# A streaming encoder layer on one core: column blocks in pairs by Strassen's algorithm, side work between the products

## The chip, the cores and the metric

The kernel runs on one core of one Trainium2 chip. The metric is the device time of one execution in microseconds. The engines are called as in the profile: PE is TensorE, DVE is VectorE, ACT is ScalarE, POOL is GpSimd, SP issues the DMAs.

## The reference

One layer of a hybrid encoder for 1088 tokens (1024 of a new stream, 64 of a running one) of width 1024. The rows of `P` are tokens; its 10,248 columns are the inputs, gates and merge gates of four branches.

```python
h = rms_norm(x, p['norm_pre'])
proj = h @ p['w_in']
lru_x, lru_g, ssd_z, ssd_xbc, ssd_dt, cf_in, cf_g, sb_qkv, sb_g, merge = split_cols(proj, IN_SPLITS)
# A: RG-LRU: causal conv of 4, two block-diagonal gates, h_t = a_t h_{t-1} + b_t; u_a = lru_h * silu(lru_g)
# B: SSD: conv of 4, silu, scan in chunks; u_b = rms_norm(y * silu(ssd_z))
# C: glu = cf_in[..., :CF_W] * sigmoid(cf_in[..., CF_W:]); conv of 31; LayerNorm; u_c = silu(...) * silu(cf_g)
# D: stick-breaking attention over the past; u_d = o * silu(sb_g)
u = jnp.stack([u_a, u_b, u_c, u_d], axis=2)
y_br = jnp.einsum('btnc,ncd->btnd', u, p['w_down'])
gates = jax.nn.sigmoid(merge.reshape(bsz, t, N_BRANCH, D_MODEL))
mixed = jnp.sum(gates * y_br, axis=2)
out = rms_norm(mixed @ p['w_out'], p['norm_post'])
return x + out, new
```

Each branch is 512 wide; `w_down` is 512 x 1024 per branch, `w_out` 1024 x 1024. The states of the scans and convolutions and k, v are outputs too.

## The kernel before

Activations lie with channels on partitions and tokens along the free axis. Every large product is done in fp32r in three parts: an operand is split into a high part (`split`: a rounding copy on ACT) and a low part (the difference, on DVE), and `mm3` (L104 to L107) adds high x high, high x low and low x high. `w_in` without dt is 80 blocks of 128 columns; `weights` (L90) loads one block of 512 KB and splits it, and `project` multiplies it with h in three pieces of tokens (`SPL`: 256, 384, 448), 24 matmuls in each piece. `proj` is that as a generator: it yields after each piece. A down product (`down`) has 12 matmuls per piece.

The order of PE is the order of the code (a manual schedule holds for PE alone); the other engines are ordered by a scheduler with priorities. A `Feed` holds generators of matrix work, and `feed.step(n)` issues n pieces of it between two steps of another chain, so that PE has something to do while that chain runs on DVE and ACT. In this order:

- head: RMSNorm of x, transposes, split into `hh` and `hl` (resident), with the first V blocks between;
- the convolution module's inputs and the attention: 68 units (`Unit.scores`, `turn`, `output`), with 18 pieces of projection per column group of k and q between them. The convolution of 31 taps runs on DVE (`conv`, L239) beside it;
- RG-LRU and the inputs of SSD (`lru_scan`, `ssd_x_chunk`), with projections between;
- LayerNorm of the convolution module (L714 on) in three pieces: mean by a ones matmul (L761), square, variance by a ones matmul (L769), root, reciprocal, scale, sigmoid, products, split, store. Between the steps stand 2 pieces of `merge` each, and `lnx` has two buffers. A piece of `merge` is a gate projection (24 matmuls) and a down product (12);
- SSD in 9 chunks (`Chunk.first` to `fourth`), pipelined over chunks: the third and fourth step of a chunk stand beside the first and second of the next, with 5 pieces of `merge` per chunk;
- the gates of the last branch (1) alone, its down products, then the output projection with RMSNorm.

`merge` computes m = sum of gate x down for the branches in the order 3, 0, 2, 1. Scratch in DRAM holds the split u of each branch (`uh_d`, `ul_d`), which `load_u` brings back in six pieces. L435 is a causal mask on POOL in the attention, L438 its scan, L439 the product after it. L742 are dt's transposes and L745 to L752 the chain from there to `adt`. L617 to L632 is `lru_scan`.

## Time and profile before

| | us |
|---|---|
| median of three runs (1494.28 to 1495.47) | 1494.86 |
| span of the profiled execution | 1490.9 |
| PE busy | 1460.1 |
| DVE busy | 921.1 |
| ACT busy | 588.5 |
| POOL busy | 118.9 |

The span is that of one profiled execution, from its first instruction to its last; the runs are timed around it. Busy time of PE is that of overlapping matmuls, so that the starts of neighbouring matmuls tell their spacing, and their durations don't. A row of a timeline has the start and the duration in us, then engine, line, operation, output <- inputs and the shape; "[a <-b]" is idle time of the engine before it and what ended that.

### The profile page before, as it was taken

How to read it: one execution, taken by the hardware profiler on the slowest of the kernel's cores; microseconds unless marked ns; L12 is line 12 of the kernel's file. 1: busy time of each engine (PE TensorE's matmuls, PEld its weight loads, DVE VectorE, ACT ScalarE, POOL GpSimd, SP SyncE). 2: the span in 40 equal slices, each digit the busy share in tenths (PEclk: the TensorE clock that was granted, in tenths of full speed). 3: DMA queues.
4: the chain of work that ended last, by engine and by line, in shares of the span. 5: the costliest groups of instructions: out<-in, count | busy, mean ns of one | idle time of the engine just before them, and what ended most of it. 6: DMA issues, size and time to landing. Idle time of an engine off the chain costs nothing.

```text
span 1490.9 us, 23008 instructions
## 1 busy us (share of the span) xinstructions
PE 1460.1 (98%) x9157; PEld 1360.5 (91%) x9157; DVE 921.1 (62%) x1379; ACT 588.5 (39%) x1000; POOL 118.9 (8%) x157
## 2 busy tenths in 40 slices
PE   6999999999999999999999999999999999999997
PEld 5898999999999998999999999999999999999885
DVE  6289589579769955677765554656655541019433
ACT  6323434443453344666644322333332332124211
POOL 0003212231221222000000000000000000000000
PEclk9999999999999999999999999999999999999999
DMA  6232212313212323454433354222621234113322
GB/s 209 75 87 63 72 61 68 103 44 89 92 46 87 98 87 109 138 117 107 116 124 116 110 169 142 82 68 83 196 78 57 75 88 148 51 43 113 99 85 71
DMA packets 103339, 144.17 MB, mean 97 GB/s; under 512 B 20800, under 2 KB 82112, under 8 KB 103232
## 3 DMA queue, kind: packets, MB, share of 16 engines
q1 hardware_dynamic: 103232, 142.71, 31.9%
q8 instruction: 72, 1.18, 0.3%
q14 instruction: 35, 0.29, 0.1%
HBM read 97.95 MB, written 40.53 MB: 93 GB/s over the span
## 4 chain that ended last, share of the span: by engine, by line
PE 87%; issue 6%; DVE 4%; DMA 1%; ACT 1%; POOL 1%; SPq 0%; DVEq 0%; POOLq 0%; ACTq 0%
PE pj L105 24%; PE pj L106 24%; PE pj L107 24%; PE pg L468 2%; PE pg L450 2%; PE pg L106 1%; PE pg L107 1%; PE pg L105 1%; DVE cvo L239 1%; PE pz L417 1%; PE pz L418 1%; PE pg L878 1%; PE pg L736 1%; PE pg L871 1%; DMA g_bc<-in_npre_dram 0%
## 5 line engine op out<-in xcount | busy, mean ns | idle before, releaser
L105 PE MATMUL pj<-hh,w_hi 128*128 128x384 f32 (+2 forms) x1920 | 637.6, 332 | 1.7 <-ACT hh L220 1.7
L106 PE MATMUL pj<-hl,w_hi 128*128 128x384 f32 (+2 forms) x1920 | 631.8, 329 | 1.8 <-DVE hl L221 1.8
L107 PE MATMUL pj<-hh,w_lo 128*128 128x384 f32 (+2 forms) x1920 | 631.5, 329 | 0.0
L105 PEld LDWEIGHTS pj<-hh,w_hi 128*128 128x128 f32 x1920 | 363.6, 189 | 16.6 <-issue 2.1
L106 PEld LDWEIGHTS pj<-hl,w_hi 128*128 128x128 f32 x1920 | 363.7, 189 | 14.4 <-DVE hl L221 2.6
L107 PEld LDWEIGHTS pj<-hh,w_lo 128*128 128x128 f32 x1920 | 363.5, 189 | 11.0
L98 DVE TENSOR_TENSOR w_lo<-w_raw,w_hi 128x1024 fp32r<-128x1024 f32 x96 | 117.5, 1224 | 226.9 <-ACT w_hi L97 226.7
L97 ACT ACTIVATE w_hi<-w_raw 128x1024 fp32r<-128x1024 f32 x96 | 101.7, 1060 | 281.7 <-PE pj L106 262.6
L239 DVE SCALAR_TENSOR_TENSOR cvo<-cbuf,p_t,cvo 128x1118 f32<-128x1118 f32 x120 | 165.6, 1380 | 2.1
L105 PE MATMUL pj<-uh,w_hi 128*128 128x384 f32 (+2 forms) x384 | 126.2, 329 | 0.0
L107 PE MATMUL pj<-uh,w_lo 128*128 128x384 f32 (+2 forms) x384 | 126.2, 329 | 0.0
L106 PE MATMUL pj<-ul,w_hi 128*128 128x384 f32 (+2 forms) x384 | 126.1, 328 | 0.0
L438 DVE TENSOR_TENSOR_SCAN fb<-fb,ones 128x128 f32<-128x128 f32 (+8 forms) x68 | 90.0, 1324 | 38.0 <-POOL fb L435 37.4
L435 POOL TENSOR_SCALAR_AFFINE_SELECT beta<-beta 128x128 f32<-128x128 f32 (+1 forms) x72 | 78.2, 1086 | 14.4 <-ACT beta L431 13.7
L698 DVE TENSOR_TENSOR sg<-pj,sg 128x256 f32<-128x256 f32 (+2 forms) x48 | 25.7, 535 | 84.9 <-PE pj L107 80.6
L689 ACT ACTIVATE sg<-pj 128x256 f32<-128x256 f32 (+2 forms) x72 | 33.7, 468 | 112.2 <-PE pj L107 112.0
L105 PEld LDWEIGHTS pj<-uh,w_hi 128*128 128x128 f32 x384 | 72.7, 189 | 2.3
L106 PEld LDWEIGHTS pj<-ul,w_hi 128*128 128x128 f32 x384 | 72.6, 189 | 2.2
L107 PEld LDWEIGHTS pj<-uh,w_lo 128*128 128x128 f32 x384 | 72.6, 189 | 2.2
L435 POOL TENSOR_SCALAR_AFFINE_SELECT fb<-fb 128x128 f32<-128x128 f32 (+1 forms) x72 | 38.2, 530 | 449.2 <-ACT fb L430 354.4
L439 DVE TENSOR_TENSOR beta<-beta,fb 128x128 f32<-128x128 f32 (+8 forms) x68 | 50.3, 740 | 4.3 <-POOL beta L435 0.7
L452 ACT ACTIVATE wT<-pg 128x512 f32<-128x512 f32 (+3 forms) x96 | 43.3, 485 | 18.1 <-PE pg L450 17.8
(313 smaller groups left out, 1683.0 us busy)
## 6 DMA issues: line engine op xcount, KB each, us to landing
w_raw<-in_win_dram SPq DMA_DIRECT2D x80, 512.0 KB, 3.7
w_raw<-in_wdn_dram SPq DMA_DIRECT2D x16, 512.0 KB, 3.6
xt<-in_x_dram SPq DMA_DIRECT2D x8, 512.0 KB, 10.5
xbc<-xs SPq DMA_DIRECT2D x8, 512.0 KB, 2.6
xb<-xbc SPq DMA_DIRECT2D x8, 512.0 KB, 4.9
w_raw<-in_wout_dram SPq DMA_DIRECT2D x8, 512.0 KB, 3.7
xr<-in_x_dram SPq DMA_DIRECT2D x8, 512.0 KB, 3.8
out_y_dram<-yo SPq DMA_DIRECT2D x16, 256.0 KB, 2.3
```

The costliest lines, as they stand in the source:

```text
L97: S.activation(hi, r3, AF.Copy)
L98: V.tensor_sub(lo, r3, hi.bitcast(FT))
L105: PE.matmul(out, ah, bh, start=first, stop=False)
L106: PE.matmul(out, ah, bl, start=False, stop=False)
L107: PE.matmul(out, al, bh, start=False, stop=last)
L239: V.scalar_tensor_tensor(out[:, :n], b[:, i:i + n], w[:, i:i + 1], out[:, :n], op0=OP.mult, op1=OP.add)
L435: G.affine_select(t_[s, 1024 - w:1024], t_[s, 1024 - w:1024], pattern=[[-1, w]], compare_op=OP.is_gt, fill=fill, base=0, channel_multiplier=1)
L438: V.tensor_tensor_scan(F[:, rev], F[:, rev], ones[:, 0:1].to_broadcast([128, n]), 1.0, OP.mult, OP.mult)
L439: V.tensor_tensor(B[:, L:1024], B[:, L:1024], F[:, L + 1:1025], op=OP.mult)
L450: PE.transpose(p[:, (j - j0) * 128:(j - j0 + 1) * 128], B[:, L + j * 128:L + (j + 1) * 128], ident)
L452: S.activation(wT[:, j0:j1, :], p[:, :(j1 - j0) * 128].rearrange("p (j c) -> p j c", c=128), AF.Copy)
L689: S.activation(sg[:, :n], p[:, :n], AF.Sigmoid)
```

## The change

**The products.** 38 pairs of column blocks (76 of the 80; all but V) are multiplied by Strassen's algorithm in Winograd's form: h is cut in four quarters (512 rows by 544 tokens), the weights of a pair into four (512 rows by 128 columns), and 7 products of a sum of weights with a sum of h take the place of 8. The sums of h are made once at the start, by DVE, and split (`quad_parts`). The sums of weights are made on POOL for each pair (`prepare`, 4 instructions), and each of the 7 weights is split (`split_w`). A product is 2 quarters of 272 tokens with 12 matmuls of 272 columns; its sums gather in PSUM banks (`bank`, 6 of them) and in two SBUF tiles R, by copies on ACT and additions on DVE. When a pair is done, `done` applies its activation and stores it to DRAM scratch; all gates are stored too (`mg_d`).

**The order.** V and dt come first, with dt's chain up to the cumulative sums (`acs`) right after them. Then 22 pairs with the inputs of all branches and the convolutions; then 16 pairs of merge gates (`NP` on), and after each of their 112 products one step of a single chain: RG-LRU in 8 items of half a channel block (17 steps), LayerNorm in 4 quarters of 272 tokens (12), SSD in 9 chunks of six steps (54), not pipelined. All tiles of these steps have one buffer, among them `xl`, `lnx`. Then the attention, with its q, k, v and gate loaded from scratch (`Head`), and between its units the 72 pieces of down products of branches 0, 2 and 1, whose gates are loaded; from the second branch on POOL adds the product to m. Last the down products of branch 3 (attention) and the output projection, as before.

The diff, cut to its core:

```diff
-LNA, LNB = (2, 2, 2), 5
...
+NSLOT, NR = 5, 3
+PV = ((0, 256), (256, 288), (544, 256), (800, 288))
...
+    V.tensor_sub(h12, h12, h11)
+    V.tensor_sub(h22, h22, h12)
+    quad_parts(6, h22)
+    V.tensor_sub(h11, h22, h11)
+    quad_parts(5, h12)
+    quad_parts(7, h11)
+    V.tensor_sub(h21, h21, h22)
+
...
+        split(hi, lo, src)
+        quad[j] = hi, lo
...
+    class Pair:
+
+
+        def __init__(self, c0, c1, done, last=AF.Copy):
+            self.chunks, self.done, self.last, self.src = (c0, c1), done, last, None
+
+        def prepare(self):
+            if self.src is not None:
+                return
+            raw = load_w(*self.chunks)
+            a11, a12, a21, a22 = raw[:, 0, 0], raw[:, 0, 1], raw[:, 1, 0], raw[:, 1, 1]
+            s1, s2, s4 = (wp.tile([128, 4, 128], FT, name=f"s{j}", bufs=1) for j in (1, 2, 4))
+            with tc.high_priority(offset=W_PRIO):
+                G.tensor_tensor(s1, a21, a22, op=OP.add)
+                G.tensor_tensor(s2, s1, a11, op=OP.subtract)
+                G.tensor_tensor(a21, a11, a21, op=OP.subtract)
+                G.tensor_tensor(s4, a12, s2, op=OP.subtract)
+            self.src = {1: a11, 6: s2, 2: a12, 7: a21, 5: s1, 4: a22, 3: s4}
...
+        def run(self, weights, between):
+            R = [ru.tile([128, T], FT, name="r", bufs=NR) for _ in range(2)]
+            banks = {}
+            for j in ORDER:
+                hi, lo = weights()
+                bh, bl = quad[j]
+                for q in range(2):
+                    key = {2: "b", 5: "c", 3: "c"}.get(j, "a"), q
+                    new = j in (1, 2, 5)
+                    if new:
+                        banks[key] = bank()
+                    p = banks[key][:, :QT]
+                    s = slice(q * QT, q * QT + QT)
+                    for k in range(4):
+                        for z, (a_, b_) in enumerate(((hi, bh), (hi, bl), (lo, bh))):
+                            PE.matmul(p, a_[:, k], b_[:, k, s], start=new and k == 0 and z == 0, stop=k == 3 and z == 2,
+                                      skip_group_check=True)
...
+                    with tc.high_priority(offset=C_PRIO):
+                        if j == 1:
+                            S.activation(r11, p, AF.Copy)
+                        elif j == 2:
+                            V.tensor_tensor(r11, p, r11, op=OP.add)
+                        elif j == 6:
+                            S.activation(r12, p, AF.Copy)
+                        elif j == 5:
+                            S.activation(r22, p, AF.Copy)
+                        elif j == 7:
+                            V.tensor_tensor(r22, p, r22, op=OP.add)
+                        elif j == 3:
+                            V.tensor_tensor(r12, p, r12, op=OP.add)
+                        else:
+                            S.activation(r21, p, self.last)
+                between()
+            self.done(R)
...
+            G.tensor_tensor(b[:, 30:TP + 30], R[0][:, :TP], R[1][:, :TP], op=OP.mult)
+            G.tensor_tensor(b[:, TP + 60:WC], R[0][:, TP:], R[1][:, TP:], op=OP.mult)
...
+    pairs = [cf(0), lx(0), q_(0), k_(0), sx(0), cf(1), lx(2), q_(2), k_(2), sx(2), cf(2), sx(4), DG[0], LG[0], cf(3), sx(6),
+             DG[1], LG[1], SZ[0], SZ[1], CG[0], CG[1]]
+    NP = len(pairs)
+    pairs += [gated(C_MG, AF.Sigmoid, mg_d, 2 * i) for i in range(16)]
...
+        for q in range(4):
+            t = slice(q * QT, q * QT + QT)
+            X = ln.tile([128, 4, QT], FT, name="lnx")
+            gl = ln.tile([128, 4, QT], FT, name="lng")
+            dma(X, cv_d[:, :, t])
+            dma(gl, cg_d[:, :, t])
+            a = fold(X)
+            yield
+            p = pg()[:, :QT]
+            PE.matmul(p, ones, a, start=True, stop=True)
+            V.scalar_tensor_tensor(X, p[:, None, :].to_broadcast([128, 4, QT]), -1.0 / 512, X, op0=OP.mult, op1=OP.add)
+            sq = ln.tile([128, 4, QT], FT, name="lnq")
+            S.activation(sq, X, AF.Square)
+            a = fold(sq)
...
+            gh = ln.tile([128, 4, QT], FR, name="lnh", tag="lnq")
+            gw = ln.tile([128, 4, QT], FR, name="lnl", tag="lng")
+            split(gh, gw, X)
+            dma(uh_d[2][:, :, t], gh.bitcast(FT))
+            dma(ul_d[2][:, :, t], gw.bitcast(FT))
+            yield
...
+                xc = lp.tile([128, HT], FT, name="xl")
+                dma(xc, xl_d[:, c, t])
+                g = lp.tile([128, HT], FT, name="lg_t")
+                dma(g, lg_d[:, c, t])
+                xh, xl = (lp.tile([128, HT], FR, name=f"xg{f}") for f in range(2))
+                split(xh, xl, xc)
+                gr = lp.tile([128, HT], FT, name="gr")
+                gx = lp.tile([128, HT], FT, name="gx")
+                yield
+                for t0 in (0, QT):
+                    for dst, w, bias in ((gr, bd[0], P("ba", c)), (gx, bd[1], P("bx", c))):
+                        p = pg()[:, :QT]
+                        mm3(p, w[0][:, c, :], w[1][:, c, :], xh[:, t0:t0 + QT], xl[:, t0:t0 + QT], True, True)
+                        S.activation(dst[:, t0:t0 + QT], p, AF.Sigmoid, bias=bias)
+                    if t0 == 0:
+                        yield
+                ga = lp.tile([128, HT], FT, name="ga")
+                S.activation(ga, gr, AF.Exp, scale=lm8[:, c:c + 1])
...
+    def between_products():
+        yield from lru()
+        yield from layer_norm()
+        yield from ssd()
+        while True:
+            yield
+
+    for n, pair in enumerate(pairs):
+        if n == NP:
+            a3.close()
+            side = between_products()
+        count = [0]
+
+        def between(n=n, count=count):
+            count[0] += 1
+            ahead(3)
+            if count[0] == 2 and n + 1 < len(pairs):
+                pairs[n + 1].prepare()
+            if n >= NP:
+                next(side)
+        pair.run(next_weights, between)
...
+        raw = wp.tile([128, 1024], FT, name="w_raw3", bufs=1)
+        dma(raw, src)
...
+    order = (0, 2, 1, 3)
...
+                if bi == 0:
+                    V.tensor_tensor(m, p[:, :n], gi, op=OP.mult)
+                else:
+                    V.tensor_tensor(gi, p[:, :n], gi, op=OP.mult)
+                    G.tensor_tensor(m, m, gi, op=OP.add)
...
-            xl = ln.tile([128, 4, NM], FT, name="lnx", bufs=2)
-            gl = ln.tile([128, 4, NM], FT, name="lng", bufs=1)
...
-    prev = None
-    feed.step(LNB)
-    for i in range(9):
-        ch = Chunk(i)
-        ch.first()
-        if prev:
-            prev.third()
-        feed.step(2)
-        if prev:
-            prev.fourth()
-        feed.step()
-        ch.second()
-        feed.step(2)
-        prev = ch
-    prev.third()
...
-    for d in range(8):
-        feed.add(proj(C_MG + 8 * b + d, act_to(sga[d], AF.Sigmoid)))
-    feed.drain()
```

Two places in the order of instructions. DVE in the LayerNorm, from the reciprocal of one piece to the start of the next; before, the second piece of 384 tokens, with `L98` the splits of weights and `L696` a merge product:

```order
L772 RECIPROCAL lnr<-lnr 128x384 [waits Activation_49]
L773 TENSOR_TENSOR lnx<-lnx,lnr 128x4x384 [waits DVE_49]
L98 TENSOR_TENSOR w_lo<-w_raw,w_hi 128x1024 [waits DMAHW7_49,PE_49,Activation_49]
L775 TENSOR_SCALAR lnx<-lnx,p_t 128x384 [waits DVE_49]
L775 TENSOR_SCALAR lnx<-lnx,p_t 128x384 x2
L98 TENSOR_TENSOR w_lo<-w_raw,w_hi 128x1024 [waits DMAHW4_49,PE_49,Activation_49]
L775 TENSOR_SCALAR lnx<-lnx,p_t 128x384
L696 TENSOR_TENSOR m_7504<-pj,sg 128x448
L777 TENSOR_TENSOR lnx<-lnx,lnq 128x4x384 [waits Activation_49]
L696 TENSOR_TENSOR m_7505<-pj,sg 128x256 [waits PE_49,Activation_49]
L778 TENSOR_TENSOR lnx<-lnx,lng 128x4x384 [waits DMAHW3_49,DVE_49]
L225 TENSOR_TENSOR lng<-lnx,lnh 128x4x384 [waits DMAHW1_49,Activation_49]
```

Now, from the second quarter of 272 tokens to the third; `L92` with `w_lo` are the splits of product weights, and `L522` is the fold of the next quarter, which waits for its load:

```order
L545 RECIPROCAL lnr<-lnr 128x272 [waits Activation_49]
L92 TENSOR_TENSOR w_lo<-w_raw,w_hi 128x512 [waits PE_49,Activation_49]
L546 TENSOR_TENSOR lnx<-lnx,lnr 128x1088 [waits DVE_49]
L548 TENSOR_SCALAR lnx<-lnx,p_t 128x272 [waits DVE_49]
L548 TENSOR_SCALAR lnx<-lnx,p_t 128x272 x3
L92 TENSOR_TENSOR w_lo<-w_raw,w_hi 128x512 [waits PE_49,Activation_49]
L550 TENSOR_TENSOR lnx<-lnx,lnq 128x1088 [waits Activation_49]
L551 TENSOR_TENSOR lnx<-lnx,lng 128x1088 [waits DMAHW7_49,DVE_49]
L92 TENSOR_TENSOR lnl<-lnx,lnh 128x1088 [waits DMAHW5_49,Activation_49]
L522 TENSOR_TENSOR lns<-lnx 128x544 [waits DMAHW4_49]
L523 TENSOR_TENSOR lns<-lns 128x272 [waits DVE_49]
L536 SCALAR_TENSOR_TENSOR lnx<-pg_7856,lnx 128x1088 [waits PE_49]
```

The next piece's fold (`lns<-lnx`, before L727, now L522) stood ahead of the reciprocal; now it stands behind the last split and a load. On PE, 146 matmuls stand between L769 and the next L761 of before, and 48 between L542 and the next L535 now.

SP's queue ahead of a down product; before, the pieces of branch 1's u, between loads of gate weights:

```order
L662 DMA ul_11871<-ul_74 128x4x384 [waits DMAHW2_49,PE_49]
L662 DMA uh_11869<-uh_70 128x4x384 [waits DMAHW3_49,PE_49]
L92 DMA w_raw<-in_win_dram 128x1024 [waits DMAHW4_49,DVE_49]
L662 DMA uh_11873<-uh_70 128x4x448 [waits DMAHW5_49,DMAHW0_49,PE_49]
L662 DMA ul_11875<-ul_74 128x4x448 [waits DMAHW6_49,DMAHW1_49]
L92 DMA w_raw<-in_win_dram 128x1024 [waits DMAHW7_49,DVE_49]
L92 DMA w_raw<-in_win_dram 128x1024 [waits DMAHW4_49,DVE_49]
L92 DMA w_raw<-in_win_dram 128x1024 [waits DMAHW7_49,DVE_49]
L92 DMA w_raw<-in_win_dram 128x1024 [waits DMAHW2_49,DMAHW0_49,DVE_49]
```

Now, the end of the queue from the last gate's store (23 issues ahead of `w_raw`; the first twelve and more are q, k and vT of the attention):

```order
L881 DMA q_s<-q_83 128x64 [waits DMAHW6_49]
L882 DMA k_s<-k_84 128x64 [waits DMAHW7_49]
L886 DMA vT_11738<-vs 128x1088 [waits DMAHW0_49]
L819 DMA ul_11742<-ul_67 128x4x384 [waits DMAHW1_49,PE_49]
L819 DMA uh_11744<-uh_63 128x4x384 [waits DMAHW2_49,Pool_49]
L819 DMA ul_11746<-ul_67 128x4x384 [waits DMAHW3_49]
L819 DMA uh_11748<-uh_63 128x4x320 [waits DMAHW4_49]
L819 DMA ul_11750<-ul_67 128x4x320 [waits DMAHW5_49]
L801 DMA w_raw_11752<-in_wdn_dram 128x1024 [waits DMAHW6_49]
L825 DMA gate<-mgs 128x1088 [waits DMAHW7_49]
L825 DMA gate<-mgs 128x1088 [waits DMAHW0_49]
```

The down weights (L801) stood among weight loads, each issued ahead of its need; the first of them now stands behind all loads of the attention and of u, which wait for PE's last product.

## Rows read from the trace of the kernel before

**Rows 1.** The page: span, busy time by engine, GB/s in 40 slices, chain
```profile
span 1490.9 us, 23008 instructions
...
PE 1460.1 (98%) x9157; PEld 1360.5 (91%) x9157; DVE 921.1 (62%) x1379; ACT 588.5 (39%) x1000; POOL 118.9 (8%) x157
...
GB/s 209 75 87 63 72 61 68 103 44 89 92 46 87 98 87 109 138 117 107 116 124 116 110 169 142 82 68 83 196 78 57 75 88 148 51 43 113 99 85 71
...
PE 87%; issue 6%; DVE 4%; DMA 1%; ACT 1%; POOL 1%; SPq 0%; DVEq 0%; POOLq 0%; ACTq 0%
```

**Rows 2.** Timeline of TensorE from 1230 us: start, duration, instruction
```profile
1230.29 0.34 PE L107 MATMUL pj<-uh,w_lo 128*128 128x384 f32 x1
...
1231.50 0.36 PE L105 MATMUL pj<-hh,w_hi 128*128 128x448 f32 x1
...
1238.93 0.28 PE L105 MATMUL pj<-hh,w_hi 128*128 128x256 f32 x1
...
1241.45 0.28 PE L105 MATMUL pj<-hh,w_hi 128*128 128x256 f32 x1
```

**Rows 3.** Groups of VectorE by shape: busy us, mean ns, idle before
```profile
L239 DVE SCALAR_TENSOR_TENSOR cvo<-cbuf,p_t,cvo 128x1118 f32<-128x1118 f32 x120 | 165.6, 1380 | 2.1
...
L225 DVE TENSOR_TENSOR uol<-yz,uoh 128x512 fp32r<-128x512 f32 x8 | 5.4, 679 | 0.0
```

**Rows 4.** Timeline of VectorE from 935 us, in a chunk of SSD
```profile
947.58 0.42 DVE L698 TENSOR_TENSOR sg<-pj,sg 128x256 f32<-128x256 f32 x1 [1.62 <-PE pj L107]
...
948.38 0.94 DVE L918 RECIPROCAL rs__9271<-rs__9271 128x128 f32<-128x128 f32 x1
949.36 1.14 DVE L920 SCALAR_TENSOR_TENSOR yz<-yz,p_t,rs__9271 128x128 f32<-128x128 f32 x4
```

**Rows 5.** Instructions of line 435 on GpSimd: ns min/median/max, first and last start
```profile
L435 POOL TENSOR_SCALAR_AFFINE_SELECT beta<-beta x72: 237/1312/2337, 116.9 to 580.4; 128x128 f32<-128x128 f32 x64, 64x64 f32<-64x64 f32 x8
```

**Rows 6.** Groups of GpSimd by shape
```profile
L808 POOL MEMSET Sb<- 128x512 f32 x2 | 1.0, 526 | 295.0 <-DVE lng L225 295.0
```

**Rows 7.** Timelines of TensorE and VectorE, the dt chain
```profile
763.68 1.02 PE L742 MATMUL pg<-ident,dtr 16*128 16x16 f32 x9
...
775.25 0.07 DVE L752 MEMSET adt<- 64x8 f32 x1
```

**Rows 8.** Timelines of TensorE and VectorE, one LayerNorm piece
```profile
817.65 0.81 PE L769 MATMUL pg<-lns,ones 128*128 128x384 f32 x2
...
835.70 1.76 DVE L225 TENSOR_TENSOR lng<-lnx,lnh 128x1536 fp32r<-128x1536 f32 x1 [1.61 <-ACT lnh L224]
```

**Rows 9.** DMA issues: destination, count, KB each, median us to landing
```profile
lg_t<-lg SPq DMA_DIRECT2D x4, 544.0 KB, 3.9
...
lnx<-cv SPq DMA_DIRECT2D x1, 768.0 KB, 7.4
```

**Rows 10.** Timelines of ScalarE and VectorE, RG-LRU of one block
```profile
621.24 0.56 ACT L617 ACTIVATE gx<-pg,p_t 128x364 f32<-128x364 f32 x1
...
627.38 1.28 ACT L622 ACT_TABLE_LOAD   x1
...
627.83 2.75 DVE L239 SCALAR_TENSOR_TENSOR xc<-abuf,p_t,xc 128x1092 f32<-128x1092 f32 x2
...
631.70 1.35 DVE L239 SCALAR_TENSOR_TENSOR xc<-abuf,p_t,xc 128x1092 f32<-128x1092 f32 x1
...
639.46 1.30 DVE L225 TENSOR_TENSOR al<-gx,ah 128x1092 fp32r<-128x1092 f32 x1
```

**Rows 11.** Timeline of SP's issues while branch 1's pieces are loaded
```profile
1231.52 0.57 SPq L662 DMA_DIRECT2D ul<-ul  x1
```

**Rows 12.** The page's costliest groups: scans and products of attention
```profile
L438 DVE TENSOR_TENSOR_SCAN fb<-fb,ones 128x128 f32<-128x128 f32 (+8 forms) x68 | 90.0, 1324 | 38.0 <-POOL fb L435 37.4
...
L439 DVE TENSOR_TENSOR beta<-beta,fb 128x128 f32<-128x128 f32 (+8 forms) x68 | 50.3, 740 | 4.3 <-POOL beta L435 0.7
```

**Rows 13.** Busy time in stretches, granted clock, DMA share, GB/s
```profile
0.00:50.00 50.00, 33.38 (x205) 30.24 (x206) 28.08 (x58) 28.03 (x52) 1.19 (x8) 0.97 0.50 171
```

More of the change, by code (lines that the diff above doesn't have):

```diff
@@ L6 @@
 from contextlib import ExitStack
-from itertools import zip_longest
 FT = mybir.dt.float32
@@ new lines, in encoder_step @@
+    for q in range(4):
+        p = pg()
+        s = slice(q % 2 * QT, q % 2 * QT + QT)
+        for k in range(8):
+            for e, b in enumerate((Bh, Bl)):
+                PE.matmul(p[:16, :QT], wd2[:, k, :], b[q // 2][:, k, s], start=k == 0 and e == 0, stop=k == 7 and e == 1)
+        S.activation(dtr[:, q * QT:q * QT + QT], p[:16, :QT], AF.Copy)
+    quad_parts(4, h21, Bh[1][:, k0], Bl[1][:, k0])
+    pd = pg()
+    for i in range(9):
+        r = 128 if i < 8 else 64
+        PE.transpose(pd[:r, i * 16:i * 16 + 16], dtr[:, i * 128:i * 128 + r], ident[:16, :16])
@@ L927, in encoder_step @@
[L927 to L945 removed]
+        u.turn()
+        if k == NU - 1:
+            u.output(None)
+    feed.drain()
+    p1.close()
     b = order[3]
```

1242 lines of the change are left out of this document (582 added, 660 removed).

## The prediction

> **What bounds the kernel now.** I read the page's busy line first, then its chain, then single instructions, then the stages that the change rebuilds. TensorE is busy for 1460.1 us of a span of 1490.9 us, and 87% of the chain that ended last is TensorE [rows 1]. So before, time is the number of matmuls times their spacing, and the side work (convolutions, RG-LRU, LayerNorm, SSD, attention) costs only what isn't covered. The three runs have a median of 1494.86 us, 4 us above the span; I forecast the span and add 4.
>
> The spacing is read from starts, not from durations, since matmuls overlap: 7 steps of 384 columns take 1.21 us, 36 steps of 448 columns 7.43 us, 21 steps of 256 columns 2.52 us [rows 2]. That is 0.173, 0.206 and 0.120 us, each 13 to 20 ns over columns divided by 2.4 GHz. A column block is 24 matmuls of each width, 24 x 0.499 = 12.0 us, and a pair of blocks 24.0 us.
>
> **The products.** A Strassen pair has 7 products x 2 quarters x 12 matmuls of 272 columns: 168 matmuls in place of 144. The nearest row is 256 columns, so 272/2.4 GHz + 13 to 20 ns = 0.127 to 0.133 us. I take the lower, by the nearer row: 24 x 0.127 = 3.06 us for a product and 21.4 us for a pair. 38 x (24.0 - 21.4) = 97 us saved; by the upper end 62 us. The plain V blocks and dt change TensorE by about +1.5 us. Net **-96**.
>
> **Phase A, 22 pairs and the convolutions (471 us of TensorE).** VectorE now has, per pair, 7 weight splits of 512 (0.68 us) and 6 additions of 272 (0.42 us by a 256-column one [rows 4]); together 7.3 us [rows 3]. The convolutions are 156 x 1.38 = 215 us as before [rows 3], and stand in the first 16 pairs. Up to there VectorE needs 215 + 16 x 7.3 + 10 (q and k splits) = 342 us against 16 x 21.4 = 342 us of TensorE: no slack. On top come 4 additions per pair on GpSimd, of two SBUF operands each, which before has nowhere. What the trace shows of GpSimd beside VectorE: the same select takes 0.24 us at least and 2.34 us at most [rows 5], which I read as waiting for a running VectorE instruction; whether VectorE waits in turn no row shows. A GpSimd instruction over 512 elements takes at least the 0.53 us of a memset [rows 6]; for the upper end I choose twice that, 1.1, since an addition reads two operands where the memset reads none. If VectorE stands still for all of it, the 64 additions of the first 16 pairs cost 34 to 70 us; if for none, 0. Later convolutions may slip into the last 6 pairs (low priority), which takes some back. I take **+30**, range 0 to 75.
>
> The Trainium skill, "SBUF — State Buffer", section "Who interferes with whom", says that a VectorE instruction with two SBUF inputs and a GpSimd instruction that reads SBUF exclude each other for the whole instruction; the spread of the select agrees for one side. "GPSIMD Engine Reference", section 3.1, has 4497 ns for a GpSimd addition of 2048 elements; a quarter of that, as an estimate, is 1.12 us for 512; with it phase A would be at about +60 and the sum 30 higher.
>
> **H to A.** The dt chain now stands with nothing between: transposes, softplus, cumulative sums. Before, the transposes start at 763.68 and the last step of dt ends at 775.32 [rows 7], 11.6 us with other work between its steps; I take off some 5 us of that and add about 2.5 for the cumulative sums that follow. **+9**, range 5 to 12.
>
> **Phase B, 16 gate pairs and the side steps.** There are 112 gaps between products and one side step in each, so 3.06 us of TensorE stands beside each step, and the steps' tiles have one buffer. The price of a step is its chain less the products beside it.
> *LayerNorm.* Before, one piece of 384 tokens takes from the matmul at 817.65 to the end of the last split at 835.70 + 1.76, 19 us after the matmul has ended at 818.46 [rows 8], hidden behind 146 matmuls of other work. A quarter of 272 is 272/384 of that, 13.5 us; then the next load can begin (one lnx buffer): 768 KB take 7.4 us [rows 9], 272/384 of it 5.2; and 1.2 us of folding. 19.9 us, and between L542 and the next L535 stand two products, 6.1 us. 13.8 x 3 quarters = 41. Entering from RG-LRU (its last split, then fold) 12, leaving to SSD, whose first VectorE rows stand behind the LayerNorm's last, 13.
> *RG-LRU.* The chain of before runs from 621.24 to 640.76 for 1092 columns, with 2.6 us of two table loads and 4.1 us of convolution in it [rows 10]; half of the rest is 6.4 us for 544 columns. Now three table loads stand in it (3.8), and a load of 256 KB into the only xl (544 KB take 3.9 us [rows 9]; 3.5 taken, and 0.6 to issue it) with its split (0.7), which stands ahead of the square root on ScalarE: 15.0. Between the gates of two items stand two products and 12 small matmuls, 7.7 us. 7.3 x 7 = 51 us, and 5 to start.
> *SSD.* One product between stages. From the norm's root to the last split before: 0.4 + 0.94 + 1.14 + two splits of 0.68 [rows 3, 4]; with the lt multiplication (0.68) that needs their tiles, a table load and hops it is 5.9 against 3.06: 2.8. The stage before it (transpose, two products of 0.68, square, two folds) 5.2: 2.2. With 0.4 elsewhere 5.4 x 9 = 48, 45 taken.
> Sum of B: 41 + 25 + 56 + 45 = **+167**, range 80 to 250 (below 80 only if the chains run at half of what the rows say).
>
> **B to C.** On SP the last gate store is followed by 24 issues up to the first down weights, all on one queue: u pieces, 12 attention loads, vT, then w_raw3. At 0.57 us each [rows 11] 14 us pass before w_raw3 is issued; the bytes are 9.3 MB, and the fullest slice moved 209 GB/s [rows 1], 44 us. The first down product needs all of this but part of u. Between 14 + 4 and 44 I take **+30**. **C to D:** branch 3 is now last, and its u pieces are stored, then loaded behind the last attention output, where before 96 us of gate projections covered that: a store and a load of 768 KB, by the 7.4 us of another load of that size [rows 9]: **+8**.
>
> **Phase C, attention with 72 down steps.** TensorE has 144 us of down products and about 143 us of attention. VectorE has 90 + 50 us of scans and products [rows 12], 38 of mixes, 15 of weight splits and outputs, 213 in all; GpSimd has its selects and 48 new additions. If these shut out VectorE for 0.5 to 1.1 us each, VectorE stays under TensorE's 287, but the units' chain scan, select, transpose has two pg buffers for three. **+20**, range 0 to 50.
>
> **The sum.** 1490.9 - 96 + 30 + 9 + 167 + 30 + 8 + 20 = 1659, plus 4 around the span: 1663 us. The output projection stays as it is. The head's new sums and splits of h (8 VectorE instructions of 2176 columns, by a 512-column one at 0.68 us about 2.9 us each at most, 23 us) stand beside 24 us of V blocks, so nothing is put down for them; without that cover they are 23.
>
> **Rivals.**
> 1. *Faster: the steps hide.* VectorE is at 62% and ScalarE at 39% [rows 1]; if the chains, without the weight splits that I scaled along, fit beside the products, B costs only its entries, 30, A and C nothing: 1491 - 96 + 9 + 30 + 30 + 8 + 4 = 1476. It is faster than 1492 only if everything outside the products sums to less than 93 us. Against: LayerNorm alone has 13.8 us a quarter uncovered by rows, and one buffer forbids starting early.
> 2. *GpSimd and VectorE stop each other for the whole of every addition,* as the spread of the select would have it: A at +75 and C at +50, 1663 + 75 = 1738.
> 3. *The clock.* With TensorE busy for 33.38 of 50 us the granted clock was 0.97 [rows 13], the level of 2.4 GHz. B would have it busy for 343 of 510 us, the same share. If it falls there to the level of 1.2 GHz, a product takes 24 x (0.227 + 0.013) = 5.8 us, and the waits shrink by what the products grow: 112 x 5.8 = 650 instead of 343 + 167, +140 at most, 1803. No row shows such a fall.
> 4. *The product is dearer,* 0.133 us a matmul: +35, 1698; inside the range.
>
> **How the numbers follow.** Forecast with its own spread (A 0 to 75, B 100 to 230, the others at their ends): 1565 to 1755, chance 0.69. Rival 1: 0.11 faster than 1492, 0.03 between 1492 and 1498, about what a measurement of this kernel can't tell from no change (0.2%). Rival 2 beyond the forecast's terms 0.10, rival 3 0.05, and 0.02 for gaps that hide half. The predicted time is the forecast's, 1663. The range, 1545 to 1765, leaves out rival 1, rival 3 and the tails. Faster 0.11, same 0.03, slower 0.86.
>
> **What would show it.** In the new trace: matmuls of a product 0.127 us apart (0.133 speaks for rival 4); phase A in 22 equal periods of 21.4 us if VectorE keeps up, longer in the first 16 if not, with GpSimd additions of 0.5 us or of 1.1 and more; waits of TensorE before L535, released by VectorE's lns, three of about 13 us; before the gate matmuls of RG-LRU about 6 us each, released by xg; in SSD before the cumulative and the norm matmul; one gap of 20 to 45 us before the first down product, ended by a DMA. Wrong it would be above all if B's waits sum to under 60, or if the granted clock falls.

## The result: 19% slower

The changed kernel takes 1779.76 us (median of 4 runs, 1776.26 to 1780.79), the kernel before 1494.57 (4 runs). The ratio is 1.190, with a 95% interval of 1.1885 to 1.1919. The forecast was 1663 us with a range of 1545 to 1765: the direction was right, the time lies above the range.

The page of the changed kernel, the lines that answer to [rows 1] and the granted clock in 40 slices:

```profile
span 1777.4 us, 26555 instructions
...
PE 1448.0 (81%) x10209; PEld 1363.0 (77%) x10209; DVE 1139.4 (64%) x1675; ACT 774.3 (44%) x1385; POOL 428.9 (24%) x365
...
PEclk9989999999999979766799888899599899989999
...
PE 48%; DVE 21%; issue 13%; ACT 7%; DMA 6%; POOL 3%; SPq 1%; DVEq 0%; POOLq 0%; ACTq 0%
```

PE's busy time is hardly less (1448.0 against 1460.1 us), although the products need some 110 us less (worked out below): at the lower clock the same matmul is busy for longer. PE now makes 48% of the chain that ended last, where it made 87%. The clock digits fall to 6 and 7 in the middle of the program and to 5 after it; in the kernel before they are

```profile
PEclk9999999999999999999999999999999999999999
```

What PE waited for, in us in total, times, and the longest (before, the longest list entry was 10.0 us in the head, and the next 2.4):

```profile
PE pg L535 <- DVE lns L523: 71.5, 4, 20.4
PE pg L676 <- DVE lt L667: 47.2, 10, 12.8
PE pj L86 <- ACT w_hi L91: 37.3, 1, 37.3
PE pg L951 <- DVE ud L983: 30.9, 16, 4.2
PE bank L394 <- DVE r L408: 29.1, 20, 3.8
PE pg L747 <- DVE yt L744: 19.4, 7, 3.7
PE pg L86 <- ACT xg L91: 19.3, 7, 3.8
PE pg L86 <- ACT gr L613: 9.6, 7, 2.3
...
PE pg L343 <- DVE adt L319: 7.6, 1, 7.6
PE pj L87 <- DMA ul<-ul: 7.5, 5, 2.5
PE pj L86 <- DMA uh<-uh: 6.1, 3, 3.7
```

L535 is the mean of LayerNorm, L676 and L747 are in SSD, L86 with xg and gr are RG-LRU's gates, L86 with w_hi is the first down product, L951 the attention's transposes, L394 the products themselves. The stages in one table (starts from PE's timeline: first and last matmul of the products, first down product), us:

| run | before the pairs | 22 pairs (A) | 16 gate pairs (B) | gap to the first down product | the rest | median |
|---|---|---|---|---|---|---|
| changed kernel | 99.6 | 507.4 | 637.3 | 37.5 | 495.6 | 1779.8 |
| filled waits (e1) | 102.2 | 506.1 | 615.7 | 37.0 | 489.3 | 1755.7 |
| two LayerNorm buffers (e2) | 99.6 | 506.8 | 620.0 | 37.3 | 493.7 | 1757.4 |
| down loads first (e3) | 100.8 | 507.0 | 638.2 | 9.1 | 521.1 | 1777.6 |
| additions on DVE (e4) | 105.7 | 465.4 | 624.9 | 37.4 | 477.8 | 1709.6 |
| plain products (e5) | 98.1 | 533.5 | 615.2 | 36.9 | 475.3 | 1761.2 |
| steps after the products (e6) | 101.6 | 507.1 | 336.6, then 402.4 with the gap | | 509.4 | 1858.9 |
| PSUM as before (e7) | 101.7 | 506.5 | 637.9 | 39.2 | 474.9 | 1759.0 |
| e4, gaps given out (e8) | 102.6 | 465.4 | 557.8 | 37.0 | 477.4 | 1645.3 |
| e8, steps first in the queues (e9) | 103.9 | 465.1 | 530.0 | 37.0 | 474.8 | 1615.0 |
| steps begin earlier (e10) | 104.6 | 537.5 | 448.5 | 8.8 | 492.8 | 1593.9 |
| e10, steps first in the queues (e11) | 103.3 | 528.8 | 439.3 | 7.8 | 495.1 | 1576.7 |

In e10 and e11 the last five of the 22 pairs already have side steps beside them, so their column A is not that of the others.

Busy time by engine, granted clock, DMA share and GB/s in A, B and the gap:

```profile
core 0: us, PE busy (x) PEld busy (x) DVE busy (x) ACT busy (x) POOL busy (x), PEclk, DMA share, GB/s
99.60:607.00 507.40, 477.82 (x3699) 472.84 (x3699) 437.59 (x516) 228.36 (x420) 190.80 (x95) 0.98 0.29 103
607.00:1244.60 637.60, 462.92 (x3234) 439.06 (x3232) 351.01 (x586) 302.07 (x477) 87.26 (x63) 0.85 0.30 99
1244.60:1281.80 37.20, 0.00 (x0) 0.00 (x0) 0.01 (x1) 1.44 (x2) 0.00 (x0) 0.55 1.05 317
```

In B, PE is at a mean granted clock of 0.85, and in the gap the DMA engines are full (317 GB/s).

### The profile page after: what moved, and what is told of

The parts are those of the page before. It is cut to its first block, busy times and chain, and to the rows that moved or that the text cites. A ratio compares the mean times of both kernels' runs of the same rounds, so it can differ in the third digit from the quotient of the medians.

```text
span 1777.4 us, 26555 instructions
## 1 busy us (share of the span) xinstructions
PE 1448.0 (81%) x10209; PEld 1363.0 (77%) x10209; DVE 1139.4 (64%) x1675; ACT 774.3 (44%) x1385; POOL 428.9 (24%) x365
## 4 chain that ended last, share of the span: by engine, by line
PE 48%; DVE 21%; issue 13%; ACT 7%; DMA 6%; POOL 3%; SPq 1%; DVEq 0%; POOLq 0%; ACTq 0%
PE bank L394 29%; DVE u L145 7%; PE pj L87 3%; PE pj L88 3%; PE pj L86 3%; DVE w_lo L92 3%; ACT w_hi L91 1%; PE pg L87 1%; POOL beta L936 1%; PE pg L86 1%; PE pg L88 1%; DMA lnx<-cv 1%; DMA ul<-ul 1%; POOL fb L936 1%; POOL m L852 1%
## 5 line engine op out<-in xcount | busy, mean ns | idle before, releaser
L394 PE MATMUL bank<-Bh,w_hi 128*128 128x272 f32 x1216 | 370.4, 305 | 29.1 <-DVE r L408 29.1
L394 PE MATMUL bank<-Bl,w_hi 128*128 128x272 f32 x1216 | 363.1, 299 | 0.0
L394 PE MATMUL bank<-Bh,w_lo 128*128 128x272 f32 x1216 | 362.0, 298 | 0.0
L394 PE MATMUL bank<-Th,w_hi 128*128 128x272 f32 x912 | 272.9, 299 | 0.4 <-ACT r L400 0.4
L394 PEld LDWEIGHTS bank<-Bh,w_hi 128*128 128x128 f32 x1216 | 242.6, 199 | 35.9 <-DVE r L408 33.7
L394 PE MATMUL bank<-Tl,w_hi 128*128 128x272 f32 x912 | 269.9, 296 | 0.0
L394 PE MATMUL bank<-Th,w_lo 128*128 128x272 f32 x912 | 268.9, 295 | 0.0
L145 DVE SCALAR_TENSOR_TENSOR u<-u,p_t 128x1118 f32<-128x1118 f32 (+1 forms) x156 | 247.4, 1591 | 10.4 <-ACT u L143 9.6
L92 DVE TENSOR_TENSOR w_lo<-w_raw,w_hi 128x512 fp32r<-128x512 f32 (+1 forms) x176 | 153.0, 872 | 144.1 <-ACT w_hi L91 139.7
L394 PEld LDWEIGHTS bank<-Bl,w_hi 128*128 128x128 f32 x1216 | 242.1, 199 | 0.9
L394 PEld LDWEIGHTS bank<-Bh,w_lo 128*128 128x128 f32 x1216 | 241.5, 199 | 0.0
L394 PEld LDWEIGHTS bank<-Th,w_hi 128*128 128x128 f32 x912 | 179.7, 197 | 2.4 <-issue 0.8
L394 PEld LDWEIGHTS bank<-Tl,w_hi 128*128 128x128 f32 x912 | 179.2, 196 | 0.6
L394 PEld LDWEIGHTS bank<-Th,w_lo 128*128 128x128 f32 x912 | 178.7, 196 | 0.0
L86 PE MATMUL pj<-uh,w_hi 128*128 128x384 f32 (+1 forms) x384 | 132.9, 346 | 43.9 <-ACT w_hi L91 37.3
L92 DVE TENSOR_TENSOR w_lo<-s,w_hi 128x512 fp32r<-128x512 f32 x114 | 85.5, 750 | 43.6 <-ACT w_hi L91 42.6
```

The lines of the kernel that those rows point to most:

```text
L86: PE.matmul(out, ah, bh, start=first, stop=False)
L92: V.tensor_sub(lo, src, hi.bitcast(FT))
L145: V.scalar_tensor_tensor(out[:, :n], b[:, i:i + n], w[:, i:i + 1], out[:, :n], op0=OP.mult, op1=OP.add)
L394: PE.matmul(p, a_[:, k], b_[:, k, s], start=new and k == 0 and z == 0, stop=k == 3 and z == 2, skip_group_check=True)
```

## The cost of the low clock, read from starts

PE after the second and longest wait of LayerNorm (start, duration in us):

```profile
778.54 1.25 PE L535 MATMUL pg<-lns,ones 128*128 128x272 f32 x2 [20.41 <-DVE lns L523]
...
780.04 0.43 PE L394 MATMUL bank<-Bh,w_lo 128*128 128x272 f32 x1
780.26 0.43 PE L394 MATMUL bank<-Bh,w_hi 128*128 128x272 f32 x1
...
783.66 0.43 PE L394 MATMUL bank<-Bh,w_hi 128*128 128x272 f32 x1
...
784.35 0.28 PE L394 MATMUL bank<-Bl,w_hi 128*128 128x272 f32 x1
784.47 0.29 PE L394 MATMUL bank<-Bh,w_lo 128*128 128x272 f32 x1
```

PE had stood for 20.41 us. After that the matmuls of 272 columns start 0.227 us apart (from 780.04 to 783.66, sixteen of them), which is 272 columns at 1.2 GHz; from 784.35 on 0.125 us, the level of 2.4 GHz. Each matmul at the lower level costs 0.1 us more. Counting the starts of each stage in this way, the lower level costs 47 us in B, 10 in A, 23 in the rest and 84 in the whole, against 20 in the kernel before. The count takes some short waits for slow matmuls: the mean granted clock of the kernel before is 0.997, which leaves some 9 us of its 1490.9 at the lower level, so that no more than about 5 us can be lost there. These figures are good to some 15 us. The Trainium skill, "TensorE: Matmul & The Clock Gate", section "HAM oscillation — how this bites in real kernels", tells the same of a kernel whose matmuls wait for loads: the clock falls in the wait, and what follows it starts cold. The trace agrees.

## The experiments

**e1: work put into the waits.** The question is whether the low clock costs time, or whether the side chains set the pace anyway.

```diff
+    def warm_up(p, n):
+        for _ in range(n):
+            PE.matmul(p[:, :QT], Bh[0][:, 0, 0:128], Bh[0][:, 1, 0:QT], start=True, stop=True)
...
             p = pg()[:, :QT]
+            warm_up(p, 112)
             PE.matmul(p, ones, a, start=True, stop=True)
```

> Edit: ahead of the matmuls of the gate pairs' side steps that wait longest, matmuls of 272 columns on operands that are always ready are issued into the same PSUM tile, which the real matmul then overwrites: 112 ahead of each LayerNorm mean, 20 ahead of each RG-LRU gate group, 24 and 16 ahead of the two SSD matmuls; 968 in all, about 122 us of PE at the full clock, put into some 170 us of waits. Nothing is left out. Theory (the fall of the granted clock after idle PE costs time of its own): the share of the gate stage at the lower level falls from about a third to under a tenth, and the time falls by 20 to 45 us, to about 1735 to 1760, although PE has 122 us more to do. Rival (the side chains on DVE and ACT alone set the pace, the clock costs nothing): 1780, or up to 40 us more where the filling overshoots.

It took 1755.67 us, 24 less. B with its clock:

```profile
608.30:1224.30 616.00, 550.40 (x4202) 529.01 (x4200) 351.22 (x586) 301.57 (x476) 87.79 (x63) 0.97 0.31 103
```

PE is busy for 550 of 616 us in B, with some 122 us more to do, and B is 21.6 us shorter than in the changed kernel; the low level's cost there falls from 47 to 20 us. So the clock costs time of its own: 27 us of slow matmuls went, and B became 21.6 us shorter. What the 20 us that are left cost isn't shown.

**e2: two buffers for LayerNorm.**

```diff
-            X = ln.tile([128, 4, QT], FT, name="lnx")
-            gl = ln.tile([128, 4, QT], FT, name="lng")
+            X = ln.tile([128, 4, QT], FT, name="lnx", bufs=2)
+            gl = ln.tile([128, 4, QT], FT, name="lng", bufs=2)
```

(and the next quarter loaded and folded ahead of the current one's root; lnl and lns get two buffers too, lnq and lnh, which share one, don't. LayerNorm has 9 steps here instead of 12, so three products fewer stand beside it)

> Edit: in the LayerNorm steps alone, two buffers for lnx, lng, lnl and lns, the next quarter loaded and folded before the current one's root, as in the kernel before. Theory (the one buffer serialises load and chain): PE's waits before the mean matmul fall from 71.5 us to 15 to 25, the time by 45 to 65 us, to about 1715 to 1735. Rival (the chain itself, delayed by ACT's table loads and POOL, sets the pace whatever the buffers): waits stay above 45 us, the time falls by under 25.

1757.38 us, 22 less. PE's waits in LayerNorm, of this run (L544 is the mean, L551 the variance):

```profile
PE pg L551 <- DVE lns L523: 45.1, 4, 16.0
...
PE pg L544 <- DVE lns L523: 17.2, 1, 17.2
```

The waits were 71.5 us before the mean; now they are 62.3, and most stand before the variance. By its numbers the rival holds, but this run doesn't show its reason, since the quarters are still kept apart by one buffer. The square that the variance needs waits for a store of the quarter before:

```profile
775.01 1.11 ACT L547 ACTIVATE lnq<-lnx 128x1088 f32<-128x1088 f32 x1 [3.47 <-DMA uh<-lnh]
```

Its input was ready at 759.8 us. The high part that is stored (lnh) lies in the one buffer of the square (lnq); three squares wait for it, and the three variance matmuls behind them 43.8 us. A second buffer there was not tried. So the load was the smaller part of the waits, and how far the chain alone exceeds its products stays open in this run.

What else delays the chain shows on ACT in the changed kernel, between the first quarter's variance matmul at 751.42 and its root at 755.95:

```profile
751.96 1.28 ACT L418 ACT_TABLE_LOAD   x1
753.26 1.11 ACT L418 ACTIVATE r<-r 128x1088 f32<-128x1088 f32 x1
...
754.66 1.28 ACT L544 ACT_TABLE_LOAD   x1
755.95 0.49 ACT L544 ACTIVATE lnr<-pg,eps_t 128x272 f32<-128x272 f32 x1
```

The activation over a finished pair's result (L418) with its table, and the table of the root behind it, stand in the queue ahead of the root. The chain of before that the prediction scaled also had an activation of a finished gate with its table in ACT's queue, at 824.28 and 825.57 us, but none between the variance matmul and the root.

**e3: the down product's loads first.**

```diff
+        nwd = weights(wdn[b, 0])
+        us = [load_u(b, 0)]
+        gates = [load_gate(b, 0)]
+        us += [load_u(b, i) for i in (1, 2)]
...
+    feed.step(3)
     heads = {0: Head(0)}
     feed.step(3)
```

> Edit: after the last gate pair the down weights and the first pieces of u and gate are issued before the attention's loads, and six down pieces instead of three stand ahead of the first attention unit. Theory (the queue of 24 issues and 9 MB ahead of the first down product makes the gap): PE's gap there falls from 37 us to 12 to 18, the time by 15 to 25 us, to about 1755 to 1765. Rival (the attention then waits for the same loads): the gap moves to the first scores, the time stays within 8 us of 1780.

1777.6 us, 2 less. The gap is 9.1 us instead of 37.5, and the rest of the program is 25.5 us longer:

```profile
PE pj L86 <- DMA uh<-uh: 14.3, 2, 8.8
PE pj L87 <- DMA ul<-ul: 13.6, 7, 2.9
PE pg L896 <- DMA vT<-vs: 10.9, 1, 10.9
```

The rival holds. The gap is a transfer: 317 GB/s for 37.2 us are 11.8 MB (the forecast counted 9.3 up to the first down weights), and in this run the order only chose which of their readers waits (u's in the down products, vT in the attention).

**e4: the additions from POOL to DVE.**

```diff
-                G.tensor_tensor(s1, a21, a22, op=OP.add)
+                V.tensor_tensor(s1, a21, a22, op=OP.add)
...
-                    G.tensor_tensor(m, m, gi, op=OP.add)
+                    V.tensor_tensor(m, m, gi, op=OP.add)
```

(so for all four of `prepare`)

> Edit: the four additions of weights per pair (152) and the additions to m in the merge (48) go from POOL to DVE. If POOL's additions shut out DVE for much of their length (convolution taps now take 1.59 us where they took 1.38, weight splits 0.87 where 0.68), taps and splits go back to 1.38 and 0.68, which gives back what the additions cost on DVE (0.68 each): time between 1765 and 1800. If POOL and DVE don't hinder each other: taps stay at 1.59, phase A gets longer by 4 x 0.68 us a pair, 35 to 45 us, and the time is 1815 to 1830.

1709.63 us, 70 less: more than the theory expected. An addition on POOL in the changed kernel (min, median, max in ns):

```profile
L374 POOL TENSOR_TENSOR s<-s,w_raw x38: 1261/1466/2383, 39.5 to 1205.2; 128x512 f32<-128x512 f32 x38
```

and a convolution tap on DVE beside it, which took 1.38 us on average before [rows 3], and at most 1.46:

```profile
L145 DVE SCALAR_TENSOR_TENSOR u<-u,p_t x156: 1340/1378/2422, 128.2 to 535.5; 128x1118 f32<-128x1118 f32 x120, 128x1092 f32<-128x1092 f32 x36
```

The groups of taps and of weight splits on DVE, in the changed kernel:

```profile
L145 DVE SCALAR_TENSOR_TENSOR u<-u,p_t 128x1118 f32<-128x1118 f32 x120 | 192.8, 1607 | 6.3 <-ACT u L143 5.5
L92 DVE TENSOR_TENSOR w_lo<-w_raw,w_hi 128x512 fp32r<-128x512 f32 x160 | 129.7, 814 | 104.3 <-ACT w_hi L91 100.1 <-DMA xl<-xls 3.4
```

and in e4, with one of the additions:

```profile
L145 DVE SCALAR_TENSOR_TENSOR u<-u,p_t 128x1118 f32<-128x1118 f32 x120 | 165.2, 1377 | 0.5
L92 DVE TENSOR_TENSOR w_lo<-w_raw,w_hi 128x512 fp32r<-128x512 f32 x160 | 109.4, 686 | 80.5 <-ACT w_hi L91 79.7
...
L374 DVE TENSOR_TENSOR s<-s,w_raw 128x512 f32<-128x512 f32 x38 | 26.0, 684 | 0.3
```

The taps are back at 1377 ns and the splits at 686, and an addition takes 684 ns on DVE where it took 1261 at least and 1466 in the middle on POOL (of the other three lines of `prepare` the middle is 1512 to 2016 and the longest 4112). In the stage of the convolutions of e4:

```profile
105.70:571.00 465.30, 465.30 (x3698) 465.30 (x3698) 418.42 (x601) 234.39 (x422) 15.80 (x11) 0.99 0.32 113
```

PE is busy throughout, and the 22 pairs take 465.4 us, 21.2 each, without a wait. DVE, with 85 instructions more in this stage (the additions), is busy for 418.4 us where it was 437.6. The two profiled spans differ by 66 us: 42 in A, 12 in B and 18 in the rest, less 6 at the start. This is what the Trainium skill, "SBUF — State Buffer", section "Who interferes with whom", says of a DVE instruction with two SBUF inputs beside a reading POOL: they exclude each other. The trace agrees, for both sides now: the longest tap (2422 ns) exceeds the shortest by 1.08 us, and POOL's addition L374 ranges from 1261 to 2383.

**e5: no Strassen.**

```diff
-            self.src = {1: a11, 6: s2, 2: a12, 7: a21, 5: s1, 4: a22, 3: s4}
+            self.src = {1: a11, 2: a12, 6: a21, 5: a22}
...
+                        for k in range(8):
+                            mm3(p, wts[k // 4][0][:, k % 4], wts[k // 4][1][:, k % 4], Bh[j][:, k, s], Bl[j][:, k, s],
+                                k == 0, k == 7)
```

> Edit on the changed kernel: the 38 pairs are multiplied plainly (192 matmuls of 272 columns a pair instead of 168, no sums of weights or of h, 4 weight splits a pair instead of 7, results copied by ACT alone), in the same order with the same steps between; the merge adds on DVE. To be set beside the run with all additions on DVE (1710), which has Strassen's products. If Strassen is worth its 24 matmuls a pair in both stages (3.0 us): the stage with the convolutions 465 + 66 = 530 us, the gate pairs + 48, less 10 us at the start: 1800 to 1820. Rival (in the gate stage the side chains set the pace, so fewer matmuls there are worth little): the gate stage grows by under 20 us, 1765 to 1790.

1761.22 us, 52 more than e4; the rival holds. A grows by 68 us, as 24 matmuls a pair should (22 x 3.0 = 66). B gets 10 us *shorter*, although PE has 48 us more to do in it. In this stage, whose pace the chains set, saving matmuls saved nothing. That the extra splits and copies which save them cost those 10 us is the likely reason, but they were not taken away alone.

**e6: the steps after the products.**

```diff
-            if n >= NP:
-                next(side)
...
+    for _ in side:
+        pass
     a2.close()
```

> Edit: the 83 side steps (RG-LRU, LayerNorm, SSD) come after the last gate pair, one behind the other, with nothing between. The gate pairs then take 16 x 21.1 = 338 us at the full clock without a wait, and what follows is the length of the chains alone. If the chains are what the waits were read as (cover 83 x 3.0 + waits 196 + small matmuls 28, so 470 us or more): 338 + 470 to 540, the whole about 1950 to 2020. Rival (the chains are short, and the products' own work on ACT, DVE and POOL is what delays them in the gate stage): under 380 us alone, the whole under 1860.

1858.9 us, from one run. The products of the 16 gate pairs, then the chains:

```profile
608.70:945.60 336.90, 336.90 (x2691) 336.90 (x2691) 120.10 (x207) 139.45 (x270) 84.15 (x61) 1.00 0.26 98
945.60:1310.00 364.40, 114.08 (x449) 73.39 (x447) 193.85 (x328) 136.80 (x175) 0.99 (x2) 0.56 0.32 99
```

The products take 336.9 us, with PE busy throughout at the full clock. The chains alone take about 365 us (402.4 less the gap of 37). Together 702 us, and laid between each other 637. In the changed kernel 28 of the 112 products come after the last step, so 84 products, 252 us, had a chain beside them, and only 65 us of that were saved. The forecast's rule (chain less products beside it) would have B at 337 + 365 - 83 x 3.0 = 453 us, if each of the 83 steps (17 of RG-LRU, 12 of LayerNorm, 54 of SSD) had one product of its own beside it. It takes 637. LayerNorm shows why, by its waits here, with nothing between:

```profile
PE pg L535 <- DVE lns L523: 81.1, 4, 20.5
...
PE pg L542 <- DVE lns L523: 15.6, 4, 3.9
```

96.7 us before L535 and L542. With 12 products, 36 us, between the steps it still waited for 71.5: here a product hid 2 us of the chain and not 3. The chain itself got longer. From the variance matmul to the end of the last split a quarter takes 14.1 us in e6:

```profile
1062.93 1.25 PE L542 MATMUL pg<-lns,ones 128*128 128x272 f32 x2 [3.90 <-DVE lns L523]
...
1075.73 1.29 DVE L92 TENSOR_TENSOR lnl<-lnx,lnh 128x1088 fp32r<-128x1088 f32 x1 [1.24 <-ACT lnh L91]
```

In the changed kernel, with the products' splits, copies and additions in the same queues, the four quarters take 20.0, 15.3, 17.5 and 18.6 us; the first ends with

```profile
770.17 1.29 DVE L92 TENSOR_TENSOR lnl<-lnx,lnh 128x1088 fp32r<-128x1088 f32 x1 [1.24 <-ACT lnh L91]
```

The rival of e6's expectation (the chains are short alone, what the products bring delays them) is the one that holds, by little: 365 us where it said under 380, and 1858.9 where it said under 1860.

**e7: PSUM banks of the attention as before.**

```diff
-        return ps.tile([128, 512], FT, name="pj3", bufs=2)
+        return ps.tile([128, 512], FT, name="pj3", bufs=3)
```

(pg3 likewise 3, pz3 1)

> Edit: in the attention stage three banks for transposes and outputs (pg) and three for down products (pj), one double bank for scores (pz), as in the kernel before, instead of two, two and two. Theory (a transposed unit waits for the bank that the output's product on DVE still holds): PE's waits before the transposes fall from 31 us to under 10, the time by 15 to 25 us to about 1755 to 1765. Rival (DVE is late, whatever the banks; or the one score bank now makes the wait): the time stays within 8 us of 1780.

1758.97 us, 21 less, all of it behind the first down product. As the theory had it: the wait before the transposes, 30.9 us, is 3.2. Half of it comes back at the one score bank:

```profile
PE pz L918 <- ACT beta L932: 16.1, 15, 2.0
```

**e8 and e9: gaps given out, queues reordered,** both on top of e4 and e2.

```diff
+                with tc.high_priority(offset=S_PRIO):
+                    next(side)
```

(e9; e8 adds yields: one in each RG-LRU item, two in 8 chunks of SSD)

> Edit: all additions on DVE; two buffers in the LayerNorm; and the 28 gaps of the gate stage that have no side step given to the steps that wait (one more product inside each RG-LRU item, two more in 8 of the 9 chunks of SSD). Theory (a step costs its chain less the products beside it, and idle PE costs clock on top): of 188 us of waits and 43 us of low clock in the gate stage some 28 x 3.0 = 84 us of waits and 20 us of clock go, the whole from 1710 to 1600 to 1630. Rival (the chains are delayed by the products' own work on the side engines, which comes with each product put between): under 40 us gained, 1670 or more.

> Edit on the run with all additions on DVE, two LayerNorm buffers and the spare gaps given out (1645): the side steps' instructions are put ahead of the products' splits and copies in the queues of ACT and DVE wherever both are ready. Theory (the chains, 365 us alone, are stretched in the gate stage because each of their instructions stands behind the products' own in the queues): PE's waits in the gate stage fall by 40 us or more, the time to 1580 to 1605. Rival (the order in the queues was right; it is the number of hops and the products that PE itself must finish first): within 10 us of 1645, or slower where the splits come late.

1645.29 us, 64 less than e4, and 1614.95, another 30. In B the waits by starts go from 188 to 132 and to 112 us, the cost of the low clock from 43 to 33 and to 29. Two waits of e8:

```profile
PE pg L551 <- DVE lns L523: 40.3, 3, 15.8
...
PE pg L690 <- DVE lt L679: 27.1, 9, 11.8
```

and the same ones of e9, one line later in the program:

```profile
PE pg L552 <- DVE lns L524: 39.9, 3, 14.4
...
PE pg L691 <- DVE lt L680: 17.0, 8, 9.3
```

Neither effect came out in full. The last matmul of the chains now stands behind 105 of the 112 products where it stood behind 84: 21 products more, 64 us, and not the 28 of the expectation (24 went to RG-LRU and SSD, and e2's form takes 3 from LayerNorm). The waits fell by 56 us where 84 were expected. How much of the 64 us of time is e2's, which took 22 alone, wasn't separated. The order in the queues, the only difference of e9 from e8, took 20 us of waits where 40 were expected. What stays is LayerNorm, 57.8 us before mean and variance in e8 and 57.7 in e9: its squares wait for the store of lnh there as in e2, and neither edit bears on that.

**e10 and e11: more gaps.** The last pairs of A are reordered so that those without a convolution stand last, and the steps begin five pairs earlier; on top of e4, e2, e3 and e7, with 18 down pieces ahead of the attention.

```diff
-    NP = len(pairs)
+    NP = len(pairs) - 5
...
-    feed.step(3)
+    feed.step(15)
     heads[0].turn()
```

> Edit: all additions on DVE; two LayerNorm buffers; the attention's PSUM banks as before; the last pairs of the first stage reordered so that those without a convolution come last, and the side steps begin five pairs earlier, so that 147 gaps stand for the same steps, the spare ones given to the steps that wait; 18 down pieces ahead of the attention, with their loads first. Theory (cover is what lacks): waits of PE beside the products fall from 132 us to 50 to 80, low clock from 33 to 15 us, 18 us come from the banks and 15 to 25 from the loads: 1500 to 1555. Rival (each added product brings its own work to the queues): waits stay above 100 us, 1575 or more.

> Edit: as the one before it, with the side steps' instructions put ahead in the queues of ACT and DVE. If the queues stretch the chains, 15 to 40 us less than it; if not, within 10 us of it.

1593.88 and 1576.65 us. The first is above its 1500 to 1555: PE's waits beside the products, by name, sum to some 89 us in e10, between the theory's 50 to 80 and the rival's 100, and nothing is seen of the 15 to 25 us from the loads: the gap and the rest together are 501.6 us, against 514.4 in e8, and e7's banks alone took 21. The second lies 17 below the first, at the lower edge of its 15 to 40. What e11 still waits for:

```profile
PE pg L87 <- ACT bdah L92: 35.8, 1, 35.8
...
PE pg L696 <- DVE lt L684: 3.0, 2, 2.8
```

SSD's wait, 47.2 us in the changed kernel, is 3.0, and from 800 us on, where SSD runs with 9 products a chunk, PE hardly waits and the clock stays:

```profile
800.00:900.00 100.00, 100.00 (x806) 97.42 (x805) 77.31 (x152) 57.83 (x98) 0.00 (x0) 1.00 0.41 131
```

The longest wait left, 35.8 us, is new: RG-LRU's first gate weights (bdah). By the program, they are loaded into memory that the convolutions hold until DVE has finished; that this is the cause was not tried. No run here is faster than the kernel before.

## The prediction, step by step

**The products, right.** 0.127 us was forecast and 0.125 to 0.126 measured; 16 pairs with nothing between them took 336.9 us (e6), 21.06 each. That is 38 x (24.0 - 21.06) = 112 us saved, forecast 97; less the 1.5 for V blocks and dt, 110.

**H to A and B to C, right** by size: 7.6 for 9, and 37.3 for 30. C to D's 8 compares with the waits for u's loads, 13.6 in all, which include the first pieces of each branch.

**Phase A.** +30 was forecast; A took 507.4 us where 465 is the products alone, +42, inside the range of 0 to 75. But the reason given was only half of it: the count put DVE at its limit (342 of 342 us), and e4 shows that DVE keeps up without a wait, with all the additions. What made A longer is that they ran on POOL.

**Phase B, the chains.** The waits as the profile names them sum to 174 us where 167 stood: LayerNorm 71.5 (forecast 41 + 12), SSD 69.2 with its entry (45 + 13), RG-LRU 33 (56). By the starts of matmuls, which also count what a wait costs until the next matmul follows at its spacing, it is 196. So the sum was nearly right for reasons that were partly wrong, which is luck: the chains alone are short (365 us for all), and the products between them lengthen them, which the rule "its chain less the products beside it" has no term for. LayerNorm shows it. Its "272/384 of that, 13.5 us" is right for the chain alone, 12.8 us in e6 from the end of the variance matmul; beside the products the same stretch took 14.7 to 19.3, and the three waits put at 13.8 were 20.4, 15.8 and 18.1.

**The clock is the step that failed.** The sum had nothing for it, because rival 3 was set aside with "No row shows such a fall" and a chance of 0.05. The row it rested on [rows 13] was a mean over 50 us, in which stretches of both levels lie: in the kernel before, matmuls of 256 columns start 0.213 us apart from 17.10 to 19.66 us, and 0.120 apart after that. Its price (140 us at most) was for a clock that stays low. What happened lies between: the level changed with the waits, and the count gives 84 us lost in slow matmuls against 20 before. Some 24 us of that are shown as time (e1). The measured span is 118 us above the forecast's 1659. By the terms used here the clock is 64 of them, B's waits 29, C with its turn to D 26, the gap 7, A 2, H to A -1 and the products -14. So the clock is the largest part and the only one that has no term in the sum; that all of its 64 us are time was not shown.

**Phase C.** +20 was forecast, and the terms beside it were seen (one bank too few, POOL's additions). Measured by taking them away, they cost 21 (e7) and 18 us (e4), so the term was half the size; the low clock of this stage comes on top.

**Rival 2** (POOL and DVE stop each other) was worked out at 75 us above the forecast. Taking POOL's additions away gives 70 us in all, some 30 of which A's term had covered. The mechanism held, beside the forecast and not instead of it; the size didn't, since A at 75 and C at 50 are more than those 70.

In one sum: the products -110, A's waits and B's waits 32 and 196, H to A and the gap 8 and 37, C and its turn to D some 54 with the waits of its small matmuls, the low clock 64 more than before: +281 of the 286.5 us by which the span grew. The terms are read from different views, and that only 5 us are left over is partly luck: B alone is 337 us of products, some 28 of small matmuls (an estimate), 196 of waits and 47 of low clock, 608 of its 637, and the 20 us counted in the kernel before are too many. What stays open: how the 47 us of low clock in B split into time lost and time that the chains would have taken anyway, since e1 fills only some of the waits; how much of LayerNorm's waits the one buffer of lnq and lnh makes; and what POOL's additions cost PE in B apart from their part in the chains.

## What to carry to other kernels

Fewer matmuls pay where PE sets the pace: the same Strassen pairs were worth 68 us beside convolutions that DVE could hide, and nothing between serial chains. A product put beside a chain hid less than its length here, because its own splits and copies stand in the same queues; putting the chain's instructions first gave 30 us (e9). So a forecast needs more products beside a chain than the chain's length alone asks for. Second buffers for some tiles of a chain don't let its pieces overlap while another tile holds them apart (e2). And the waits of PE were paid a second time in slow matmuls after them, so a forecast of waits needs a term for the clock.
